# Twelve of the mixer's sixteen gate tiles as block products: seven products in place of eight, and the modulation rows moved

## The chip, the cores and the metric

The kernel runs on one core of a Trainium2 chip. The metric is the device time of one execution in microseconds, the median of several runs. One profiled execution gives the trace that is read here. Times inside the trace count from the start of its span.

## The reference

One decoder block over 512 tokens of width 1024, in float32. Three sub-layers follow each other, each behind an RMSNorm that is modulated by rows of `cond @ w_ada` (9 x 1024 values): a SwiGLU feed-forward part, a token mixer, a second feed-forward part; then a last RMSNorm.

```python
mod = cond @ w_ada[l] + b_ada[l]                       # nine vectors: shift, scale, gate, three times
u = modulate(rmsnorm(h, g_norm_ffn1[l]), sh1, sc1)
h = h + 0.5 * gt1 * swiglu(u, w_ffn1_in[l], w_ffn1_out[l])
u = modulate(rmsnorm(h, g_norm_mix[l]), sh2, sc2)
h = h + gt2 * token_mixing(u, ...)
...
# token_mixing
proj = u @ w_in                                        # pool 256, q 768, k 768, v 768, gates 2 x 1024
...
gates = sigmoid(gate_logits); g_pool, g_attn = split(gates, 2)
merged = g_pool * (y_pool @ w_pool_branch) + g_attn * (y_attn @ w_attn_branch)
return merged @ w_out
```

The gates are 2048 columns of `u @ w_in`: sixteen tiles of 128 columns, eight for `g_pool` and eight for `g_attn`.

## The kernel before

**Layout and precision.** Activations lie transposed: 1024 features as eight tiles of 128 partitions by 512 tokens. A float32 product is made of three matmuls: every operand is split into a hi part and a lo part, and `mm3` (L340) multiplies hi by hi, hi by lo and lo by hi into one PSUM bank. So a tile of 128 output columns (`mm_tile`, L1011) takes 8 x 3 matmuls of 512 columns. `UH` and `UL` hold the two parts of the normalised input, `MH` and `ML` those of the merged tiles.

**Weights.** Every weight chunk (128 x 1024 float32, 512 KB) is fetched by a DMA on SP's queue (`fetch`, L218) into one of three buffers `raw`, and is then split: `split_hi` (L274) lets ScalarE copy it to a ring `whi`, `split_lo` (L305) lets VectorE subtract that and write `wlo`. `look(n)` (L320) issues the splits n chunks ahead of the one that is taken. The buffer comes free when VectorE has done the lo part. The order in which the program is written is the order on every engine; the engines run on by themselves and wait for each other's results.

**Block products.** Most of the two feed-forward parts already use a scheme with seven products instead of eight (`duo`, L733): features and tokens are cut in two halves, four weight tiles in four blocks r11, r12, r22, r21, and sums and differences of the blocks are multiplied. A product (L720) has 24 matmuls of 256 columns. The sums of the weights are made by VectorE (`make`, L237) when a chunk is split; the order of a duo's seven entries is written in `blocks` (L167): r11, x0 = r12 - r11, x1 = r22 - x0, r21, r12 - r22, r22, x0 = r21 - x1. The sums of the activations are made once per sub-layer and split into `S`. Three PSUM banks A, B, C collect the seven products in the order A, B, A, C, A, B, A, and ScalarE copies A out (to C, to an SBUF tile) between the products. A settling matmul (L348) of 240 columns stands where matmuls of 512 columns give way to matmuls of 256.

**The mixer** (`mix`, L1195) goes: four q/k tiles of the first attention group together with the norm (`head`), the first group's values, eight q/k tiles of the dilated groups, two pool tiles, four value tiles, four gate tiles, then `merge_out` (L1327). Attention is hung into these tiles by `hooks` (L1259): at the sixth of the eight k steps of a tile stand the values of the block before last, the transposes of the last one, the scores of the next one and its softmax (maxima on VectorE, exponentials on ScalarE). Behind each q/k tile stands the rope (`rope_a`, L993: ScalarE copies the bank, four DMAs on SP's queue swap halves, VectorE multiplies by the cosine; `rope_b`, L1005: VectorE multiplies the swapped half by the sine and adds), its second half at the seventh step of the tile after.

**The merge.** `merge_out` makes the other twelve gate tiles, two for each merged tile m, each with `mm_tile`, and for every m the branches: twelve matmuls of 512 columns into two banks, then on VectorE two multiplications with the gates (L1355, L1356) and an addition (L1357), on ScalarE the hi part (L1358), on VectorE the lo part (L1359). Then comes the last product, `merged @ w_out`, with the out tail (`out_tail`).

**Modulation rows.** The 72 rows of 128 values of `mod` are made by VectorE, one instruction per row over a 512 KB tile of `w_ada` (`ada_do`, L364), fetched on SP's queue (`ada_fetch`, L357). `bg` (L388) does one row and fetches the next. Rows 48 to 71 are made in `merge_out`, two beside each of the twelve gate tiles, from a pool of four buffers. `AR` and `cs` are two 128 x 1024 tiles that hold norm sums and the rope's cosine and sine.

## Time and profile before

| what | us |
|---|---|
| time, median of 3 runs (997.77 to 998.7) | 998.47 |
| the profiled execution | 998.29 |
| its span in the trace | 996.5 |
| TensorE busy | 988.0 |
| VectorE busy | 746.8 |
| ScalarE busy | 456.9 |
| GpSimd busy | 26.8 |

The granted clock of TensorE was 1.00. In the rows of a timeline the columns are: start in us, duration in us, engine, line of the program, operation, output and inputs, shapes, count; in brackets the idle time of the engine ahead of it and what ended that. A matmul's duration is that of its pipelined passage; the distance of two starts is its price. In rows that sum a window: its length, then busy time and count for TensorE, its weight loads, VectorE, ScalarE and GpSimd, then the granted clock, the DMA share and GB/s. In rows of DMA issues: count, KB each, median us from issue to landing.

### The profile page before, as it was taken

What the parts mean: (1) busy time and instruction counts of PE and PEld (TensorE: products, weight loads), DVE (VectorE), ACT (ScalarE), POOL (GpSimd) and SP (SyncE); (2) the same over time, 40 slices, a digit from 0 to 9 for tenths busy, and PEclk for the clock granted to TensorE, in tenths of its full rate; (3) what the DMA queues carried; (4) which work ended last, traced back from release to release, by engine and by line L of the source; (5) the groups of instructions that cost most, each with busy time, mean ns of one, the idle gap of its engine ahead of it and who ended that gap; (6) DMA issues with size and microseconds to landing.
All of it is one profiled execution on the core that took longest, in us unless ns stands there. A gap on an engine that the chain in (4) does not pass through costs nothing.

```text
span 996.5 us, 15853 instructions
## 1 busy us (share of the span) xinstructions
PE 988.0 (99%) x6467; PEld 889.3 (89%) x6467; DVE 746.8 (75%) x1051; ACT 456.9 (46%) x690; POOL 26.8 (3%) x31
## 2 busy tenths in 40 slices
PE   9999999999999999999999999999999999999997
PEld 7888999989999999788878888998899899998997
DVE  7989979889797675776457776568797776676764
ACT  5443643625444454356432323464355254352553
POOL 0000000000000000008000000000000000000002
PEclk9999999999999999999999999999999999999999
DMA  9856446354564314433146663312343234241312
GB/s 345 276 195 224 149 149 210 134 197 160 190 186 124 120 61 123 127 104 119 44 148 241 233 236 125 106 65 81 111 149 128 64 107 147 86 148 43 105 45 85
DMA packets 44873, 141.70 MB, mean 142 GB/s; under 512 B 6273, under 2 KB 9089, under 8 KB 44802
## 3 DMA queue, kind: packets, MB, share of 16 engines
q1 hardware_dynamic: 44226, 140.18, 42.5%
q8 instruction: 50, 0.82, 0.3%
q10 hardware_dynamic: 576, 0.52, 0.2%
q14 instruction: 21, 0.17, 0.0%
HBM read 135.29 MB, written 2.24 MB: 138 GB/s over the span
## 4 chain that ended last, share of the span: by engine, by line
PE 95%; DVE 2%; DMA 1%; issue 1%; POOL 0%; ACT 0%; SPq 0%; POOLq 0%; DVEq 0%; ACTq 0%
PE bank L342 17%; PE bank L343 17%; PE bank L344 17%; PE bank L729 11%; PE bank L730 11%; PE bank L731 11%; PE bank L1541 2%; PE bank L1543 1%; PE bank L1545 1%; PE bank L1046 1%; PE bank L1305 1%; PE bank L1097 1%; PE bank L1306 1%; PE bank L1307 1%; PE bank L1079 1%; DMA H<-xT 1%
## 5 line engine op out<-in xcount | busy, mean ns | idle before, releaser
L311 DVE TENSOR_TENSOR wlo<-raw,whi 128x1024 fp32r<-128x1024 f32 (+5 forms) x171 | 175.7, 1040 | 65.6 <-ACT whi L299 64.9
L299 ACT ACTIVATE whi<-raw 128x1024 fp32r<-128x1024 f32 (+5 forms) x171 | 150.4, 898 | 47.3 <-DVE raw L243 43.9
L729 PE MATMUL bank<-UH,whi 128*128 128x256 f32 x544 | 150.2, 276 | 0.0
L730 PE MATMUL bank<-UL,whi 128*128 128x256 f32 x544 | 150.2, 276 | 0.0
L731 PE MATMUL bank<-UH,wlo 128*128 128x256 f32 x544 | 150.2, 276 | 0.0
L342 PE MATMUL bank<-HI,whi 128*128 128x512 f32 (+1 forms) x406 | 146.2, 360 | 0.0
L343 PE MATMUL bank<-HK,whi 128*128 128x512 f32 (+1 forms) x406 | 145.9, 359 | 0.0
L344 PE MATMUL bank<-HI,wlo 128*128 128x512 f32 (+1 forms) x406 | 145.8, 359 | 0.0
L342 PE MATMUL bank<-UH,whi 128*128 128x512 f32 (+1 forms) x400 | 143.0, 358 | 0.0
L343 PE MATMUL bank<-UL,whi 128*128 128x512 f32 (+1 forms) x400 | 141.6, 354 | 0.1
L344 PE MATMUL bank<-UH,wlo 128*128 128x512 f32 (+1 forms) x400 | 141.4, 354 | 0.0
L311 DVE TENSOR_TENSOR wlo<-X,whi 128x1024 fp32r<-128x1024 f32 (+4 forms) x101 | 111.8, 1112 | 32.1 <-ACT whi L299 31.9
L729 PE MATMUL bank<-SH,whi 128*128 128x256 f32 x408 | 112.7, 276 | 0.0
L730 PE MATMUL bank<-SL,whi 128*128 128x256 f32 x408 | 112.6, 276 | 0.0
L731 PE MATMUL bank<-SH,wlo 128*128 128x256 f32 x408 | 112.6, 276 | 0.0
L299 ACT ACTIVATE whi<-X 128x1024 fp32r<-128x1024 f32 (+4 forms) x101 | 95.5, 966 | 34.2 <-DVE X L243 33.5
L729 PEld LDWEIGHTS bank<-UH,whi 128*128 128x128 f32 x544 | 102.1, 188 | 0.3
L730 PEld LDWEIGHTS bank<-UL,whi 128*128 128x128 f32 x544 | 102.1, 188 | 0.0
L731 PEld LDWEIGHTS bank<-UH,wlo 128*128 128x128 f32 x544 | 102.1, 188 | 0.0
L344 PEld LDWEIGHTS bank<-HI,wlo 128*128 128x128 f32 x406 | 76.2, 188 | 11.7
L342 PEld LDWEIGHTS bank<-HI,whi 128*128 128x128 f32 x406 | 76.2, 188 | 11.5
L343 PEld LDWEIGHTS bank<-HK,whi 128*128 128x128 f32 x406 | 76.3, 188 | 11.3
(252 smaller groups left out, 1714.0 us busy)
## 6 DMA issues: line engine op xcount, KB each, us to landing
ada<-wada SPq DMA_DIRECT2D x47, 512.0 KB, 5.4
raw<-wmix SPq DMA_DIRECT2D x44, 512.0 KB, 3.7
raw<-wf1i SPq DMA_DIRECT2D x31, 512.0 KB, 4.3
raw<-wf2i SPq DMA_DIRECT2D x30, 512.0 KB, 3.6
X<-wf2i SPq DMA_DIRECT2D x14, 512.0 KB, 3.9
cs<-wada SPq DMA_DIRECT2D x12, 512.0 KB, 3.5
AR<-wada SPq DMA_DIRECT2D x12, 512.0 KB, 4.1
X<-wf1i SPq DMA_DIRECT2D x12, 512.0 KB, 4.4
```

The costliest lines, as they stand in the source:

```text
L299: self.nc.scalar.activation(self.hi[:, y], r[:, x], AF.Copy)
L311: self.nc.vector.tensor_tensor(self.lo[:, y], r[:, x], self.hi[:, y], op=OP.subtract)
L342: M(ps, hi, uh, start=start, stop=False)
L343: M(ps, hi, ul, start=False, stop=False)
L344: M(ps, lo, uh, start=False, stop=stop)
L729: M(o, hi, uh, start=start and p == 0 and k == 0, stop=False, skip_group_check=True)
L730: M(o, hi, ul, start=False, stop=False, skip_group_check=True)
L731: M(o, lo, uh, start=False, stop=k == 3, skip_group_check=True)
L1046: nc.tensor.matmul(S[:, o], q[:, toks], k[:, ks], start=True, stop=True, skip_group_check=True)
L1079: nc.tensor.transpose(b[:, i * P:i * P + P], p[:, i * P:i * P + P], self.ident)
L1097: self.nc.tensor.matmul(self.bO[64 * h:64 * h + 64, P * hp:P * hp + P], x, pt[:, (2 * h + j) * P:(2 * h + j + 1) * P], start=j == first, s ...
L1541: M(b, hi, self.UH[k], start=k == 0, stop=False)
```

## The change

Merged tiles are made in the order 6, 7, 0, 1, 2, 3, 4, 5. Tiles 6 and 7 have their four gate tiles as before, ahead of the merge. For the pairs (0, 1), (2, 3), (4, 5) the four gate tiles become one `gate_duo`: a settling matmul and seven products, with a copy of the feed-forward's bank scheme and two sigmoid tiles `gs` and `gc` for the four gates. The weights of these tiles are laid out as blocks. In `merge_out` a fourth `raw` buffer is added and `AR` and `cs` serve as x0 and x1. The activation sums are made by `mix_sums` in ten steps, which stand as hooks in the last value tile and three gate tiles; their tiles take the place of q, k and v tiles that are no longer read, as do the merged tiles. The pool that held the modulation rows' buffers in the merge is gone: rows 48 to 64 are made beside attention (one per q/k tile and in the first pool tile, two in the second pool tile and in three value tiles; buffer `AR`, from the second pool tile on also `cs`), rows 65 to 71 behind the first five tiles of the last product.

```diff
@@ lay_mix, plan
-    for m in range(KT + 1):
-        if m < KT:
-            ch.append(_fmajor(w_in, 2560 + np.arange(m * P, (m + 1) * P)))
-            ch.append(_fmajor(w_in, 3584 + np.arange(m * P, (m + 1) * P)))
...
+    for j in MERGED[::2]:
+        if j < KT - 2:
+            ch.extend(_blocks(w_in, *GATES, j))
...
+MERGED = (6, 7, 0, 1, 2, 3, 4, 5)
+GATES = (2560, 3584)
...
-        plain(mx)
+        plain(mx[:26])
+        for i in range(26, len(mx) - KT, 6):
+            blocks(mx[i:i + 4])
+            plain(mx[i + 4:i + 6])
+        plain(mx[-KT:])
@@ mix_sums (new): ten steps on VectorE and ScalarE, and last()
+        def last():
+            u = x[0].rearrange("p (k t) -> p k t", k=4)
+            nc.scalar.activation(self.S[3][0], u, AF.Copy)
+            sub(self.S[3][1], u, self.S[3][0])
...
+        return [lambda: whole(b, 0, 1), lambda: whole(x[0], 4, 1),
+                lambda: (v.tensor_tensor(x[0], x[0], b, op=OP.add), hi(0)), lambda: whole(x[1], 0, 0),
+                lambda: sub(x[2], x[1], b), lambda: (sub(x[1], x[0], x[1]), lo(0)),
+                lambda: (hi(2), whole(x[0], 4, 0)), lambda: (hi(1), sub(x[0], x[0], x[1])), lambda: lo(2), lambda: lo(1)], last
@@ mix
+            self.ada_free, self.ada_stop, self.ada_depth = [self.AR], 65, 2
+            self.bg_fetch()
...
-                        b = self.mm_tile(hooks(todo.pop(0), rest))
+                        b = self.mm_tile(hooks(todo.pop(0), rest + [(7, self.bg)]))
...
-            b = self.mm_tile(hooks([], rest + [(6, lambda: by_class(0))]))
+            b = self.mm_tile(hooks([], rest + [(6, lambda: by_class(0)), (7, self.bg)]))
             self.pool_diff(0, b)
-            b = self.mm_tile(hooks(g23[0], [(2, lambda: by_class(1))]))
+            self.ada_free.append(self.cs)
+            self.bg_fetch()
+            b = self.mm_tile(hooks(g23[0], [(2, lambda: by_class(1)), (3, self.bg), (7, self.bg)]))
...
-                hk = hooks(g23[c + 1], (), mid) if c < 3 else hooks([], [(2, self.at_swap)])
+                hk = hooks(g23[c + 1], [(2, self.bg), (7, self.bg)], mid) if c < 3 else \
+                    hooks([], [(2, self.at_swap), (2, nxt), (3, nxt), (6, nxt), (7, nxt)])
...
-            gates.append(self.mm_tile({6: [self.pool_map, lambda: self.at_fT(self.bS[1])]}))
+            gates.append(self.mm_tile({1: [nxt], 3: [nxt], 6: [self.pool_map, lambda: self.at_fT(self.bS[1])]}))
...
@@ gate_duo (new)
+        for i, (bank, u, start) in enumerate(((A, lambda: blk(lo4, T1), True), (B, lambda: S(0), True),
+                                              (A, lambda: S(1), False), (C, lambda: blk(hi4, T1), False),
+                                              (A, lambda: S(2), False), (B, lambda: S(3), False),
+                                              (A, lambda: blk(hi4, T2), False))):
+            if i == 6:
+                v.tensor_tensor(q(c, 1), q(c, 1), r(p5), op=OP.add)
+            self.look(4)
+            self.product(bank, u(), start, not i)
+            if i == 0:
+                copy(C, A)
+                if last:
+                    last()
+            elif i == 1:
+                copy(p5, B)
+            elif i == 2:
+                copy(q(c, 0), r(A))
+            elif i == 3:
+                sig(q(s, 0), r(C))
+            elif i == 4:
+                copy(q(c, 1), r(A))
+            elif i == 6:
+                sig(q(s, 1), r(A))
+                v.tensor_tensor(q(c, 0), r(B), q(c, 0), op=OP.add)
+        sig(c, c)
@@ merge_out
-            for m in range(KT):
-                if 0 < m < KT - 1:
-                    for _ in range(2):
-                        gates.append(sig(self.mm_tile()))
-                        self.bg()
-                        self.bg()
...
+            p5, raw = mg.tile([P, T], F32, name="p5"), mg.tile([P, D], F32, name="raw")
+            self.free.append(raw)
+            self.X, self.retired = [self.AR, self.cs], []
+            self.ready = True
...
+            for j in MERGED[::2]:
+                if j < 6:
...
+                    self.gate_duo(*sc, p5, last)
+                    last = None
+                for m in (j, j + 1):
...
+                    branch(m)
...
+            self.ada_free, self.ada_stop = [ma.tile([P, D], F32, name=x) for x in ("k0", "k2")], 72
+            self.bg_fetch()
...
                 self.sumsq(m, self.H[m])()
+                self.bg()
+                if m < 2:
+                    self.bg()
```

`branch(m)` is the body of the former loop over m, from `look()` to the lo part.

## The prediction

> **What bounds the kernel now.** I read the page first (shares, then the chain that ended last), then the timelines of the mixer's last third, engine by engine.

> ```profile
> PE 988.0 (99%) x6467; PEld 889.3 (89%) x6467; DVE 746.8 (75%) x1051; ACT 456.9 (46%) x690; POOL 26.8 (3%) x31
> ...
> PE 95%; DVE 2%; DMA 1%; issue 1%; POOL 0%; ACT 0%; SPq 0%; POOLq 0%; DVEq 0%; ACTq 0%
> ```

> TensorE is busy for 99% of the span and makes up 95% of the chain: nearly every microsecond of matmul that goes is a microsecond of time, and nearly every new wait of TensorE is one too. No other engine is near its limit on average, so the question is where the changed order makes TensorE wait. The price of a matmul, from the timeline of TensorE, in the mixer's merge and in the second feed-forward part:

> ```profile
> 520.07 0.39 PE L342 MATMUL bank<-UH,whi 128*128 128x512 f32 x1
> ...
> 530.95 0.39 PE L342 MATMUL bank<-PH,whi 128*128 128x512 f32 x1
> ...
> 716.45 0.27 PE L348 MATMUL bank<-UH,whi 128*128 128x240 f32 x1
> 716.56 0.28 PE L729 MATMUL bank<-UH,whi 128*128 128x256 f32 x1
> ...
> 735.61 0.28 PE L729 MATMUL bank<-UH,whi 128*128 128x256 f32 x1
> ```

> From 520.07 to 530.95 stand two gate tiles, 48 matmuls of 512 columns: 0.2267 us each (the 0.39 of a row is the pipelined length, not the price). From 716.56 to 735.61 stands one duo, the seven block products: 168 matmuls of 256 columns in 19.05, 0.1134 each, 2.72 a product. The 240-column settling matmul in front of it takes 0.11.

> **1. The removed matmuls.** Three times, four gate tiles (96 x 0.2267 = 21.76) become a settling matmul and a duo (19.16). Saved: 3 x 2.60 = 7.8 us, all on the path. The built program has 219 matmul instructions more, which is 3 x (168 - 96 + 1): the change does what it says. The weights are as many bytes as before.

> **2. A new wait in each gate duo.** In `gate_duo`, product 0 is accumulated in bank A, ScalarE copies A to C, and product 2 accumulates onto A again: it must wait for that copy. The copy is queued on ScalarE behind the two weight splits that `look(4)` issued ahead of product 0 (`branch` had looked ahead by 3 only). The second of them reads r12-r22, a subtraction that VectorE has behind the last `ML` of the branch before. Feed-forward 1 shows the same link once, at its first duo:

> ```profile
> 111.41 1.22 DVE L243 TENSOR_TENSOR X<-X 128x1024 f32<-128x1024 f32 x1
> ```
> ```profile
> 112.67 1.07 ACT L299 ACTIVATE whi<-X 128x1024 fp32r<-128x1024 f32 x1 [1.72 <-DVE X L243]
> 113.63 0.58 ACT L736 ACTIVATE u<-bank 128x512 f32<-128x512 f32 x1
> ```
> ```profile
> 114.27 0.38 PE L729 MATMUL bank<-SH,whi 128*128 128x256 f32 x1
> 114.49 0.28 PE L730 MATMUL bank<-SL,whi 128*128 128x256 f32 x1
> ```

> Subtraction to split 1.26, split to copy 0.96, copy 0.58 long, TensorE 0.06 after its end; and the first matmul after the wait takes 0.22 instead of 0.11. What comes ahead of the subtraction is read from a branch of the kernel as it is, which ends on TensorE at 547.27:

> ```profile
> 547.27 0.39 PE L342 MATMUL bank<-UH,whi 128*128 128x512 f32 x1
> ```
> ```profile
> 547.47 0.69 DVE L1356 TENSOR_TENSOR sg<-sg,bank 128x512 f32<-128x512 f32 x1 [0.22 <-PE bank L344]
> 548.19 0.69 DVE L1357 TENSOR_TENSOR sg<-sg 128x512 f32<-128x512 f32 x1
> 549.59 0.69 DVE L1359 TENSOR_TENSOR ML<-sg,MH 128x512 fp32r<-128x512 f32 x1 [0.70 <-ACT MH L1358]
> 550.54 1.23 DVE L311 TENSOR_TENSOR wlo<-raw,whi 128x1024 fp32r<-128x1024 f32 x1 [0.26 <-ACT whi L299]
> 551.68 1.22 DVE L369 SCALAR_TENSOR_TENSOR ada<-ada,cond 128x1024 f32<-128x1024 f32 x1
> ```
> ```profile
> 548.92 0.63 ACT L1358 ACTIVATE MH<-sg 128x512 fp32r<-128x512 f32 x1 [2.99 <-DVE sg L1357]
> 549.46 1.05 ACT L299 ACTIVATE whi<-raw 128x1024 fp32r<-128x1024 f32 x1
> ```

> Counted from the end of the pair's first branch: second multiplication at 0.20, `MH` 1.65, `ML` 2.32; the next chunk's lo part must wait for its hi part, queued on ScalarE behind `MH`, so it starts at 3.27 and leaves VectorE free at 4.41. The second branch ends at 2.72, but VectorE takes its first multiplication only at 4.41, the second 0.61 later at 5.02; then, by the same steps, `MH` at 6.47, `ML` at 7.14, the subtraction at 7.74, the split at 9.00, the copy from 9.96 to 10.54, TensorE at 10.60. Product 2 could start at 2.72 + 0.11 + 2 x 2.72 = 8.27. Wait: 2.33 + 0.11 = 2.4 us, in the second and third duo. At the first it is longer. There ScalarE has a table load and four sigmoids to do first, and in the kernel as it is takes its next split at

> ```profile
> 518.65 0.65 ACT L299 ACTIVATE whi<-raw 128x512 fp32r<-128x512 f32 x1
> ```

> In the changed one this is chunk r12-r11 and its lo part stands ahead of the branch's multiplications: 518.65 + 1.08 + 1.14 = 520.87 for the first, 521.48 for the second, against 520.07 + 0.20: 1.2 later. So 3.6. The three: 8.4 us. Floor, if the lo part does not hold VectorE up: the second multiplication at 2.92, 0.3 a duo, 1.0 in all. Later products have margins: the other copies stand behind one split each; the copy of product 2, worked out the same way, has 0.5 us left in the first duo and 2 in the others. As a bound on throughput VectorE is not it: a group takes 11 operations of 1.14 (551.68 less 550.54) and 12 of about 0.61, 19.9 us, of 19.16 + 5.44.

> **3. Modulation rows beside attention.** 17 rows, each a 512 KB DMA on SP's queue and one VectorE instruction of 1.22 (row 551.68), now stand at the end of the q/k tiles, with one buffer (AR) until the pool tiles. On SP the row's DMA waits for VectorE to be done with the row before, and the four rope DMAs of the tile (L1000) are queued behind it. Rope's second half waits for those, and the next row stands behind that on VectorE: a loop.

> ```profile
> 397.64 2.41 SPq L1000 DMA_DIRECT2D rt<-tr  x4
> 400.16 0.52 SPq L227 DMA_DIRECT2D raw<-wmix  x1
> 403.09 2.41 SPq L1000 DMA_DIRECT2D rt<-rt  x4
> ```
> ```profile
> 401.64 0.69 DVE L1008 TENSOR_TENSOR rt<-rt,cs 128x512 f32<-128x512 f32 x1 [1.79 <-DMA rt<-tr]
> 402.37 1.09 DVE L1009 TENSOR_TENSOR q<-q,rt 128x512 f32<-128x512 f32 x1
> 403.39 1.05 DVE L1002 TENSOR_TENSOR q<-bank,cs 128x512 f32<-128x512 f32 x1
> ```
> ```profile
> AR<-wada SPq DMA_DIRECT2D x12, 512.0 KB, 4.1
> ```

> Issue of a 512 KB row 0.5 (row 400.16), rope DMAs to rope 4.0 (397.64 to 401.64; I take 3.9, since four issues are done after 2.41), rope's two steps 1.75, the row 1.22: 7.4 us a turn. The first row that is late ends at 401.64 + 1.75 + 1.22 = 404.6, six turns later at 449.0, and the last rope starts 4.4 after that, at 453.4, and ends at 455.2. The next row then runs to 456.4, and the one after it stands at k = 3 of the second pool tile, in the same buffer: its DMA lands 4.1 later, at 460.5, it ends at 461.7. Behind it on VectorE stands the softmax of the first dilated scores.

> ```profile
> 454.35 1.09 PE bank L1046 x16
> ...
> 461.19 0.88 PE bank L1079 x8
> ```
> ```profile
> 455.47 0.42 DVE L1062 CUSTOM_DVE_ANT_0 prob<-bank,masks 128x256 f32<-128x256 f32 x1 [1.55 <-PE bank L1046]
> ```
> ```profile
> 458.49 0.50 ACT L1067 ACTIVATE prob<-prob,negmax 128x256 f32<-128x256 f32 x1
> ```

> The scores (454.35) would wait 0.9 for the rope. The last exponential ended 3.5 after VectorE's first maximum (455.47 to 458.99): now at 465.2. The second half of the transposes was due at 461.6. Wait in all 3.6, the 0.9 in it. Floor: nothing, if a turn takes no longer than a tile (from 403.09, the end of the second q/k tile, to the scores at 454.35, five of eight steps into the tenth tile, lie 7.6 tiles, 6.7 us each). Upper end: if the rope's pieces land only when the 512 KB in front of them has, a turn grows by about 1 us, and seven turns and the last row by 8: 12. I take 3.6; the loop's terms are all rows.

> **4. The rest, at nothing.** The ten steps of `mix_sums` (eleven VectorE instructions of 1.14, three of ScalarE) lie beside the last value tile and three gate tiles:

> ```profile
> 468.00:496.00 28.00, 28.00 (x200) 23.37 (x199) 12.14 (x32) 13.46 (x28) 5.98 (x6) 1.00 0.16 49
> 496.00:513.00 17.00, 17.00 (x81) 12.46 (x80) 10.01 (x23) 4.15 (x8) 0.00 (x0) 1.00 0.33 101
> ```

> VectorE is idle there for 23 of 45 us; the steps take 12.5, the rows of the value tiles 8. Cover gone: about 1 us at the transposition of the merge factors. The last seven rows stand behind the first five tiles of the last product; the third and fourth wait some 3 us for their buffers, but the weights of the next four tiles (5.4 us each) are split by then. The 24 rows that leave the merge give nothing back by themselves: TensorE did not wait there.

> **Sum.** -7.8 + 8.4 + 3.6 = +4.2 us. The profiled execution took 998.29 (span 996.5, 1.8 outside it), 0.18 under the median of 998.47; forecast 998.47 + 4.2 = 1002.7. About 0.2%, 2 us, can be told from no change.

> **Rivals.**
> A, the forecast, 45%: 1002.7, own range 999.5 to 1006.
> B, rows and ropes land in time and attention doesn't wait: +0.6, 999.1. For it: 6.7 us a tile against 7.4 a turn is a close call. 19%.
> C, the rope's pieces queue behind the rows' bytes: attention waits 6 to 12, 1005 to 1011. For it: one queue; against it: a row lands 4.1 after its issue, about when the last rope piece would land anyway. 9%.
> D, TensorE waits nowhere new: 998.47 - 7.8 = 990.7, the faster side. Mechanism: VectorE takes the second branch's multiplications without waiting for the lo part, and the copy comes in time; it decides at 2.3 us of slack a duo, and attention's at 3.6. For it: TensorE waits nowhere now, and at the one place shown the feed-forward duo loses 0.1. 13%.
> E, only the duos are at their floor: -7.8 + 1.0 + 3.6, 995.3. 11%.
> F, a wait makes the granted clock fall, 3%:

> ```profile
> 991.00:995.00 4.00, 0.10 (x1) 0.00 (x0) 1.76 (x6) 0.39 (x1) 1.41 (x2) 1.00 0.75 254
> ```

> Here TensorE has nothing to do from 991.10 on and the clock is still 1.00 at 995: 3.9 us idle did no harm, more than either long wait (3.6). Were it halved during one product after each of the two, that is 2 x 2.7 us more: 1008. [...]

> **How the numbers follow.** Faster by over 0.2%: D and E, 0.24. Within: most of B and the low end of A, 0.21. Slower: the rest, 0.55. The range leaves out D and the upper half of C: 994 to 1008; the likeliest case's own is given above.

> **What would show it.** Right: seven products of 19.05 a duo; a wait of TensorE for ScalarE's copy at the first matmul of the third product in each duo, 3.6, 2.4, 2.4; a wait at the first transposes of dilated attention, with a VectorE row waiting for its DMA just ahead. Wrong: no such waits, a copy that ends before product 1 does, or matmuls of 256 columns at more than 0.1134. A new wait in the last product or at the merge factors would upset step 4.

## The result and the profile after

The changed kernel took 1019.96 us (median of 4 runs, 1018.91 to 1021.9) against 998.23 for the kernel before: ratio 1.022, interval 1.0202 to 1.0238. It is slower by 21.7 us where 4.2 were forecast, and outside the range. The profiled execution (1021.9, span 1020.1) shows the same: 23.6 us more span. All windows and waits below are of that execution unless another kernel is named.

The page, shares and chain:

```profile
PE 993.1 (97%) x6686; PEld 900.9 (88%) x6686; DVE 788.6 (77%) x1091; ACT 475.6 (47%) x713; POOL 30.2 (3%) x31
...
PE 85%; DVE 6%; ACT 3%; DMA 2%; issue 2%; SPq 1%; POOL 0%; POOLq 0%; DVEq 0%; ACTq 0%
```

TensorE's share of the chain fell from 95% to 85%; VectorE, ScalarE and the DMAs have taken the rest. So there are places now where TensorE waits for them. The waits of TensorE (total us, times, longest):

```profile
PE bank L742 <- ACT bank L1396: 7.7, 3, 3.5
PE bank L1091 <- DVE k L1054: 4.5, 1, 4.5
PE bank L1142 <- DVE v L1375: 3.0, 1, 3.0
PE bank L1124 <- ACT prob L1112: 2.6, 2, 2.0
```

The first row is the three gate duos, the other three are attention: the scores that wait for the rope, the values that wait for VectorE's copy of the first value tile, the transposes that wait for the softmax. And behind some waits the granted clock is lower (window, its length, busy times of the engines, then the granted clock):

```profile
446.60:449.90 3.30, 3.30 (x9) 2.56 (x8) 3.30 (x5) 1.87 (x3) 0.00 (x0) 0.50 0.10 10
466.50:470.40 3.90, 3.90 (x10) 3.08 (x10) 2.64 (x3) 0.00 (x0) 3.75 (x4) 0.50 0.37 119
...
547.90:551.50 3.60, 0.16 (x2) 0.00 (x0) 3.47 (x4) 2.65 (x6) 0.00 (x0) 1.00 0.01 2
551.60:555.60 4.00, 4.00 (x22) 4.00 (x23) 3.66 (x4) 3.00 (x4) 0.00 (x0) 0.60 0.27 66
...
580.90:584.90 4.00, 4.00 (x36) 4.00 (x37) 4.00 (x4) 3.37 (x5) 0.00 (x0) 1.00 0.32 74
```

In the wait from 547.90 on TensorE does nothing and the clock reads 1.00; in the 4 us behind it, when the matmuls are back, it reads 0.60, with 22 matmuls of 256 columns where 36 fit (the window after the second duo's wait). When exactly it falls is shown at the experiment clock.

Where the 23.6 us come from, by setting the starts of the same matmuls in both traces side by side:

| part | us |
|---|---|
| removed matmuls (as forecast) | -7.8 |
| three waits in the duos, 3.7, 2.4, 2.1, and 0.1 for each restart | +8.6 |
| four waits in attention, 2.2, 4.7, 0.7, 3.1 | +10.7 |
| transposes one by one behind the exponentials, 0.9 twice | +1.8 |
| lower clock behind the waits: 5.4 in attention, 1.6 behind the first duo's | +7.0 |
| some products of 256 columns at 118 ns a matmul in place of 113 | about +2.6 |
| not assigned | about +0.7 |

The loss of the transposes is no matter of the clock, which reads 1.00 there. Eight of them, first in the kernel before, then in the changed one:

```profile
441.14 1.04 PE L1079 MATMUL bank<-cst,prob 128*128 128x128 f32 x8
```
```profile
444.56 1.92 PE L1124 MATMUL bank<-cst,prob 128*128 128x128 f32 x8 [2.04 <-ACT prob L1112]
```

In the changed kernel two of them start every 0.49 us, as far apart as the exponentials that they read (443.91, 444.42, 444.91 and 445.40 on ScalarE).

### The profile page after: what moved, and what is told of

Read it like the earlier page. It is cut to its first block, busy times and chain, and to the rows that moved or that the text cites. A ratio compares the mean times of both kernels' runs of the same rounds, so it can differ in the third digit from the quotient of the medians.

```text
span 1020.1 us, 16353 instructions
## 1 busy us (share of the span) xinstructions
PE 993.1 (97%) x6686; PEld 900.9 (88%) x6686; DVE 788.6 (77%) x1091; ACT 475.6 (47%) x713; POOL 30.2 (3%) x31
## 4 chain that ended last, share of the span: by engine, by line
PE 85%; DVE 6%; ACT 3%; DMA 2%; issue 2%; SPq 1%; POOL 0%; POOLq 0%; DVEq 0%; ACTq 0%
PE bank L355 13%; PE bank L356 13%; PE bank L357 13%; PE bank L742 12%; PE bank L743 12%; PE bank L744 12%; PE bank L1669 1%; PE bank L1671 1%; PE bank L1673 1%; DMA rt<-rt 1%; ACT whi L312 1%; DVE AR L382 1%; DVE wlo L324 1%; SPq L1045 1%; DMA rt<-tr 1%
## 5 line engine op out<-in xcount | busy, mean ns | idle before, releaser
L324 DVE TENSOR_TENSOR wlo<-raw,whi 128x1024 fp32r<-128x1024 f32 (+4 forms) x168 | 175.3, 1056 | 54.3 <-ACT whi L312 53.7
L742 PE MATMUL bank<-UH,whi 128*128 128x256 f32 x640 | 177.2, 277 | 0.0
L743 PE MATMUL bank<-UL,whi 128*128 128x256 f32 x640 | 177.2, 277 | 0.0
L744 PE MATMUL bank<-UH,wlo 128*128 128x256 f32 x640 | 177.1, 277 | 0.0
L312 ACT ACTIVATE whi<-raw 128x1024 fp32r<-128x1024 f32 (+4 forms) x168 | 149.9, 910 | 51.7 <-DVE raw L256 47.6
L324 DVE TENSOR_TENSOR wlo<-X,whi 128x1024 fp32r<-128x1024 f32 (+3 forms) x104 | 111.8, 1083 | 32.4 <-ACT whi L312 32.1
L312 ACT ACTIVATE whi<-X 128x1024 fp32r<-128x1024 f32 (+3 forms) x104 | 95.8, 943 | 33.6 <-DVE X L256 32.9
L355 PE MATMUL bank<-UH,whi 128*128 128x512 f32 (+1 forms) x304 | 107.2, 353 | 0.0
L356 PE MATMUL bank<-UL,whi 128*128 128x512 f32 (+1 forms) x304 | 105.8, 348 | 0.1
L357 PE MATMUL bank<-UH,wlo 128*128 128x512 f32 (+1 forms) x304 | 105.6, 347 | 0.0
L356 PEld LDWEIGHTS bank<-HK,whi 128*128 128x128 f32 x406 | 76.3, 188 | 11.3
## 6 DMA issues: line engine op xcount, KB each, us to landing
raw<-wmix SPq DMA_DIRECT2D x44, 512.0 KB, 3.8
raw<-wf1i SPq DMA_DIRECT2D x31, 512.0 KB, 4.5
raw<-wf2i SPq DMA_DIRECT2D x30, 512.0 KB, 4.1
AR<-wada SPq DMA_DIRECT2D x25, 512.0 KB, 4.2
ada<-wada SPq DMA_DIRECT2D x23, 512.0 KB, 5.7
cs<-wada SPq DMA_DIRECT2D x16, 512.0 KB, 3.6
X<-wf2i SPq DMA_DIRECT2D x14, 512.0 KB, 3.7
X<-wf1i SPq DMA_DIRECT2D x12, 512.0 KB, 4.4
```

The lines of the kernel that those rows point to most:

```text
L312: self.nc.scalar.activation(self.hi[:, y], r[:, x], AF.Copy)
L324: self.nc.vector.tensor_tensor(self.lo[:, y], r[:, x], self.hi[:, y], op=OP.subtract)
L355: M(ps, hi, uh, start=start, stop=False)
L356: M(ps, hi, ul, start=False, stop=False)
L357: M(ps, lo, uh, start=False, stop=stop)
L742: M(o, hi, uh, start=start and p == 0 and k == 0, stop=False, skip_group_check=True)
```

## The experiments

Times are medians, with the ratio to the kernel before, run in turn on the same chip (998.4 to 999.0). Single runs of one changed kernel differ by up to 0.6%, those of the kernel before by up to 0.3%.

**no_rows: attention without the rows.**

```diff
+            if not 48 <= j < 65:
                 self.nc.sync.dma_start(t[:, c], self.a["wada"][j * P:(j + 1) * P, c])
...
+            x = self.cond if 48 <= j < 65 else t
+            if 48 <= j < 65:
+                c = slice(0, 32)
```

> The 17 modulation rows beside attention are left out: their DMAs are gone and their VectorE instruction works on 32 columns of another tile (rows 48 to 64 of mod are not computed). Theory (the rows are the whole of attention's loss): the aligned traces lose 18.1 us between the first dilated q/k tiles and the merge; all of it goes, 1020.0 - 18.1 = 1001.9, own range 1000.5 to 1003.5, no wait of TensorE over 0.8 us in attention, granted clock 1.00 there. The duos keep their waits of 3.7, 2.4 and 2.1. Rival (the ten steps of the activation sums, or VectorE's load as such, hold a part): attention keeps 4 us or more, over 1006.

1003.22 us (1.0041, 1.0029 to 1.0053). The profiled run has no wait in attention; the duos' stay:

```profile
PE bank L746 <- ACT bank L1400: 7.7, 3, 3.5
```

By the starts of the same matmuls the changed kernel loses 18.3 us in attention against the kernel before, and no_rows loses nothing there. So all of it is the rows' doing, and the sums of `mix_sums` cost TensorE nothing there.

**rope_first: the same rows, another order on the queue.** `bg(False)` does a row and fetches none:

```diff
-                        b = self.mm_tile(hooks(todo.pop(0), rest + [(7, self.bg)]))
+                        b = self.mm_tile(hooks(todo.pop(0), rest + [(7, lambda: self.bg(False))]))
                         rt = [self.scratch(2 * i + hp)[:, :T] for i in range(2)]
                         self.rope_a(b, dst, hp, 4, *rt)
+                        self.bg_fetch()
```

> Only the order on the DMA queue: beside the eight dilated q/k tiles the four rope DMAs are issued ahead of the next row's fetch. Theory 1 (the loop through the queue): the rope no longer waits for the row before it, a tile keeps its 6.7 us, the waits at 442 (2.2) and 461 (4.7) go with the lower clock behind each (2.3 and 2.1): 1020.0 - 11.3 = 1008.7, 1006.5 to 1011; the waits at 474 (0.7) and 483 (3.2) stay. Theory 2 (VectorE has no time for a row in a q/k tile, whatever the queue does): the waits stay within 1 us, 1018 to 1021. Theory 3 (a row that comes later holds VectorE up instead): a VectorE row waits over 1 us for its DMA in each tile, 1012 to 1018.

1005.63 us (1.0068, 1.0051 to 1.0084): 14.3 less, where theory 1 gave 11.3; of the 3.0 more, 1.6 is the wait at 474, which went too (0.7, and 0.9 at its transposes). One wait stays in attention, 3.2 at the value tile. SP's queue and VectorE's rows, first of the changed kernel, then of rope_first:

```profile
423.30 0.33 SPq L374 DMA_DIRECT2D AR<-wada  x1
423.74 2.41 SPq L1045 DMA_DIRECT2D rt<-rt  x4
...
431.78 0.33 SPq L374 DMA_DIRECT2D AR<-wada  x1
```
```profile
428.79 0.69 DVE L1053 TENSOR_TENSOR rt<-rt,cs 128x512 f32<-128x512 f32 x1 [1.30 <-DMA rt<-rt]
...
430.52 1.22 DVE L382 SCALAR_TENSOR_TENSOR AR<-AR,cond 128x1024 f32<-128x1024 f32 x1
```
```profile
426.11 2.41 SPq L1046 DMA_DIRECT2D rt<-tr  x4
428.62 0.53 SPq L374 DMA_DIRECT2D AR<-wada  x1
```
```profile
430.06 0.69 DVE L1054 TENSOR_TENSOR rt<-rt,cs 128x512 f32<-128x512 f32 x1 [0.77 <-DMA rt<-tr]
...
432.20 1.23 DVE L382 SCALAR_TENSOR_TENSOR AR<-AR,cond 128x1024 f32<-128x1024 f32 x1 [0.33 <-DMA AR<-wada]
```

In the changed kernel a fetch comes every 8.48 us (423.30, 431.78), and the rope's pieces land 5.05 after their issue (423.74 to 428.79). With the rope first they land after 3.95 (426.11 to 430.06), the loop is broken, and theory 2 falls: VectorE has time for a row in a tile of 6.7 us. Theory 3 is seen but small: the row waits 0.33 for its DMA.

**eighth: the same order, an eighth of the bytes.**

```diff
+            if 48 <= j < 65:
+                c = slice(0, D // 8)
             self.nc.sync.dma_start(t[:, c], self.a["wada"][j * P:(j + 1) * P, c])
```

> The DMAs of the 17 rows beside attention bring an eighth of the row (64 KB in place of 512 KB), at the same place of the queue; VectorE's instruction keeps its size but reads another tile (rows 48 to 64 of mod are not computed). Theory 1 (bytes: the rope's pieces land late because 512 KB go ahead of them): the pieces land 3.9 to 4.1 us after the first issue, not 5.05, the turn of the loop falls from 8.45 to the 7.4 that was forecast; the wait at 461 shrinks from 4.7 to about 1 to 2 us, that at 442 to under 1, with less of the lower clock: 1005 to 1010. Theory 2 (the order of issue alone counts, not the bytes): the turn stays at 8.3 or more, 1017 to 1021.

1010.85 us (1.0128, 1.0102 to 1.0154), slightly above theory 1's range. In its trace:

```profile
427.30 0.33 SPq L376 DMA_DIRECT2D AR<-wada  x1
427.73 2.41 SPq L1048 DMA_DIRECT2D rt<-tr  x4
...
434.64 0.33 SPq L376 DMA_DIRECT2D AR<-wada  x1
```
```profile
431.68 0.69 DVE L1056 TENSOR_TENSOR rt<-rt,cs 128x512 f32<-128x512 f32 x1 [2.27 <-DMA rt<-tr]
```

The pieces land after 3.95, a turn takes 7.34: the loop as it was forecast (7.4), to 0.1. So the missing 1.1 us a turn is the 512 KB in front of the pieces, and TensorE's wait for the rope falls from 4.7 to 1.2; 1.9 at the transposes behind it take a part of that back.

**attn_fix: no rows before the first value tile's copy.** rope_first, and three rows moved into the gate tiles:

```diff
-            b = self.mm_tile(hooks(g23[0], [(2, lambda: by_class(1)), (3, self.bg), (7, self.bg)]))
+            b = self.mm_tile(hooks(g23[0], [(2, lambda: by_class(1)), (7, self.bg)]))
...
-                hk = hooks(g23[c + 1], [(2, self.bg), (7, self.bg)], mid) if c < 3 else \
+                hk = hooks(g23[c + 1], [(2, self.bg), (7, self.bg)] if c else [], mid) if c < 3 else \
...
```

> rope_first, and three rows moved: none at step 3 of the second pool tile and none in the first value tile; one each in the first three gate tiles. Theory (the 3.2 us that rope_first still lost stand for the rows ahead of VectorE's copy of the first value tile): that wait goes, 1005.6 - 3.2 = 1002.4, own range 1000.5 to 1004, the same as with no rows at all (1003.2). Rival (what waits there is GpSimd's pooling, which makes VectorE's instructions 2.1 long in place of 1.2, and not the rows): 1 to 2.5 us of it stay, 1003.5 to 1005.

1005.04 us (1.0068, 1.0054 to 1.0082): 0.6 less than rope_first, hardly a gain, and yet attention is clean, as with no rows at all. The time went to the next place where VectorE is full:

```profile
PE bank L743 <- ACT bank L1401: 10.9, 3, 6.7
```

The first duo's wait is 6.9 in place of 3.7: the rows in the gate tiles held up VectorE's steps ahead of the first branch. What VectorE does in the value tile of the changed kernel is shown by these rows:

```profile
478.81 2.08 DVE L382 SCALAR_TENSOR_TENSOR AR<-AR,cond 128x1024 f32<-128x1024 f32 x1
...
484.87 1.22 DVE L382 SCALAR_TENSOR_TENSOR cs<-cs,cond 128x1024 f32<-128x1024 f32 x1
...
486.01 0.69 DVE L1375 COPY v<-bank 128x512 f32<-128x512 f32 x1
```

The copy that TensorE waits for stands behind two rows, 2.08 and 1.22; with them moved away its wait of 3.2 is gone. The rival (GpSimd's pooling is the cause, and not the rows) falls, since the pooling runs in attn_fix too. But it may have a share: beside its first operations (L1214, 477.88 to 484.05 on GpSimd) the first row takes 2.08 where the second, behind them, takes 1.22, and a split between the two 2.06 where others take 1.22, together up to 1.7 of the wait.

**copy_first: ScalarE's copy ahead of the splits.**

```diff
-            self.look(4)
+            self.look(4 if i else 2)
             self.product(bank, u(), start, not i)
```

> Only the gate duo's order: product 0 looks 2 chunks ahead, not 4, so that ScalarE's copy of bank A stands ahead of the two splits. Theory (the copy behind the splits is the whole of the wait): the three waits (3.7, 2.4, 2.1), their restarts (0.3) and the time at a lower clock after the first (1.9) go, 10.3 us: 1009.7, own range 1008.5 to 1011. Rival (the wait only moves: the two splits come too late for products 3 and 4): a wait of 1 to 3 us at the first matmul of product 3 or 4 in each duo, 1013 to 1019.

1016.65 us (1.0181, 1.0166 to 1.0197): 3.3 less, not 10.3. Its waits in the duos:

```profile
PE bank L742 <- ACT gc L1396: 1.7, 3, 1.1
PE bank L744 <- DVE wlo L324: 1.3, 1, 1.3
...
PE bank L742 <- ACT bank L1396: 0.5, 1, 0.5
```

The waits at product 2 fell to 0.64, 0.47 and 0.44, so the splits were most of them, but in the first duo 1.4 and 1.3 came back at products 3 and 4, as the rival said. Starts of matmuls set side by side give 6.0 us for the duos in the two profiled runs; attention, with the same code, lost 2.5 more in this one than in the other.

**branch_look: the lo part out of the gap between the branches.**

```diff
-                self.look()
+                self.look(3 + (m % 2 == 0))
                 w = self.take()
                 pb, ab = self.nb(), self.nb()
```

> The changed kernel with one edit: the first branch of a pair looks 4 chunks ahead, so that VectorE's lo part of the second one no longer stands between the two branches; the two splits stay ahead of the copy. Theory (as forecast, the lo part between the branches is 1.5 us of each wait, the splits ahead of the copy the rest): the waits of the second and third duo fall from 2.4 and 2.1 to about 0.9 and 0.6; at the first, where VectorE starts late, the lo part only changes its place and 3.7 becomes 2.2 to 3.7; in all 3 to 6 us less, 1014 to 1017. Rival (the copy's own place behind the splits is nearly all): the waits stay above 1.8, 1019 to 1020.

1023.29 us (1.0245, 1.023 to 1.0261): both sides missed, it is 3.3 slower than the changed kernel. The waits are 3.3, 2.8 and 2.5, and the third now has 1.6 at a lower clock behind it. Ahead of the second duo's branches:

```profile
568.38 1.06 ACT L1404 ACTIVATE gc<-gc 128x1024 f32<-128x1024 f32 x1 [0.27 <-DVE gc L1427]
569.35 1.04 ACT L312 ACTIVATE whi<-cs 128x1024 fp32r<-128x1024 f32 x1
```
```profile
570.42 1.23 DVE L324 TENSOR_TENSOR wlo<-cs,whi 128x1024 fp32r<-128x1024 f32 x1 [2.07 <-ACT whi L312]
571.57 0.68 DVE L1455 TENSOR_TENSOR gs<-gs,bank 128x512 f32<-128x512 f32 x1
```

The lo part now waits for a hi part that stands behind the sigmoid of the duo before, VectorE is idle for 2.07, and the first branch starts at 571.57, 2.6 later than in the changed kernel against the same duo. What was taken out between the branches was put in ahead of both.

**duo_fix: the edits of copy_first and branch_look, and `last()` behind product 2.** The third edit:

```diff
                 copy(C, A)
-                if last:
-                    last()
             elif i == 1:
                 copy(p5, B)
             elif i == 2:
                 copy(q(c, 0), r(A))
+                if last:
+                    last()
```

> The gate duo again, with three orders changed: the copy of bank A ahead of the splits (as before), the weights of the second branch of a pair split ahead of the first branch's steps (the first branch looks 4 ahead), and the in-place sum that last() makes moved from product 0 to product 2. Theory (the wait is a queue: copy behind MH behind VectorE's lo part between the branches; copy_first took away only the splits): TensorE waits under 0.3 us at product 2 of each duo and under 0.3 at products 3 and 4, and the clock stays at 1.00 there: 10.3 us less than the changed kernel, 1009.7, own range 1008 to 1011.5. Rival (VectorE's load: it has 19.9 us of work in a group of 24.6 and the wait comes back wherever its queue is longest): 0.5 to 1.5 us a duo stay, 1012 to 1016.

1016.86 us (1.0172, 1.0155 to 1.0189), the rival's side, 0.9 above its range, and no better than copy_first. Set side by side the duos gain 6.2 us in the profiled run (1013.11, the fastest of the four); 2.9 of waiting are left, and they are ScalarE's copies behind splits once more, now also at product 4:

```profile
PE bank L742 <- ACT gc L1398: 1.9, 3, 0.7
PE bank L742 <- ACT bank L1398: 1.0, 2, 0.7
```

**both, best2, best3, best4: the whole computation, step by step.** `both` is duo_fix with attn_fix; the others move the rows on, and from best3 on the look-ahead of a duo's product is issued behind the copy that follows it (this edit alone is shown):

```diff
-            self.look(4 if i else 2)
             self.product(bank, u(), start, not i)
...
+            self.look()
         sig(c, c)
```

> duo_fix and attn_fix together, the whole computation done. Theory (the two waits and the lower clock behind them are all that stands against the removed matmuls): 1020.0 - 10.3 - 17.6 = 992.1; from the other side 998.5 - 7.8 = 990.7; so 990.5 to 993, faster than the kernel before by 0.6%. Rival (the waits share a cause, or a further one shows once they are gone): 995 to 1000.

999.76 us (1.0008, 0.9999 to 1.0017). Attention is clean; the first duo waits 3.8 for the three rows in the gate tiles, with 1.6 at a lower clock. The waits do share VectorE's time, so the rival holds.

> As both, but the three rows that both had in the gate tiles now stand behind the third to fifth tile of the last product (two rows per tile there). Theory (in both the three rows held VectorE up ahead of the first duo: its first branch was multiplied 2.8 us after TensorE's end, and TensorE waited 3.8 with 1.6 at a lower clock behind it): the first duo's wait falls to the 0.7 of duo_fix; 999.8 - 4.7 = 995.1, own range 993.5 to 996.5. Rival (the rows cost as much behind the last product, where VectorE has the weights of the last tiles to split): 997 to 1000.

1002.57 us (1.0033, 1.002 to 1.0045), worse, above both ranges. The first duo's wait at product 2 is cured (0.3), but the norm behind the last product waits 3.7 for VectorE, and a matmul of the last product 1.3 for a lo part.

> As best2, and in the gate duo the splits of each product's look-ahead are issued behind the copy that follows the product, not ahead of the product. Theory (the waits of 0.5 to 0.9 that duo_fix still had at product 4, and of 0.7 at product 2, are ScalarE's copies behind splits again): 2.5 of the 2.9 us left in the duos go, 1.5 to 3 us below best2, 991 to 994: faster than the kernel before by 0.5 to 0.8%. Rival (the splits come too late for their products instead): a wait for VectorE's lo part, no gain on best2.

998.71 us (1.0004, 0.9995 to 1.0013): 3.9 below best2, more than the 1.5 to 3 that were expected, and still above the range. The duos wait no more than 0.4 each. What is left:

```profile
PE bank L446 <- DVE AR L553: 2.8, 1, 2.8
```

This is the norm behind ten rows in the last product, and 1.2 at a lower clock behind it.

> As best3, with the modulation rows spread otherwise after attention: two in the third gate duo (behind products 4 and 6, in tiles of S that are read no more), eight behind the last product's first five tiles (best3 had ten there), three buffers. Theory (what best3 still loses, 3.0 us at the norm behind the last product and 1.2 at a lower clock behind it, is VectorE's backlog of ten rows): the wait falls below 0.7, 998.7 less 3 to 4.2: 994.5 to 995.7, faster than the kernel before by 0.3 to 0.45%. Rival (rows in the third duo bring its waits back): 996 to 999.

993.49 us (0.9947, 0.9934 to 0.9959): faster than the kernel before by 4.9 us, 26 less than the change as it was made, and 1.0 below the range. Its page:

```profile
PE 982.8 (99%) x6686; PEld 894.1 (90%) x6686; DVE 787.9 (79%) x1091; ACT 475.0 (48%) x713; POOL 29.5 (3%) x31
...
PE 88%; DVE 6%; ACT 2%; DMA 2%; issue 1%; POOL 0%; SPq 0%; POOLq 0%; ACTq 0%; DVEq 0%
```

TensorE is busy for 99% of the span again, with the same work on every engine. 2.9 us of the 7.8 are still missing. TensorE's waits of over 0.15 in the gate and merge part add up to 1.4 (0.3 and 0.4 in the first two duos, 0.7 at the start of the last product), and matmuls of 256 columns at 118 ns cost about 1.1 more than in the kernel before; the rest was not traced further.

**clock: what a wait costs behind it.** The kernel before, with n further copies on ScalarE in each duo of the second feed-forward part:

```diff
             if i == 0:
+                for _ in range((7, 8, 9, 10, 11, 12, 8, 9, 10, 9, 10)[j // 2] if hasattr(self, "f2") else 0):
+                    copy(p5, A)
                 copy(C, A)
```

> The kernel before, with 7, 8, 9, 10, 11, 12, 8, 9, 10, 9, 10 further copies of bank A on ScalarE ahead of the copy in the eleven duos of the second feed-forward part (their result is overwritten): TensorE waits about 1.6, 2.1, 2.6, 3.1, 3.6, 4.1, 2.1, 2.6, 3.1, 2.6, 3.1 us for it. Theory 1 (a length decides: so far a wait of 3.7 was always followed by matmuls at half speed for about 4 us, one of 2.1 never): all waits over about 3 are followed by it, none under 2.4. Theory 2 (the place in a grid of fixed windows decides, since waits of 2.4 were followed by it once in four): among the waits of 2.1 to 3.1 some are and some are not, without order in their length. Theory 3 (it is not the wait but what TensorE does after it): none is.

Nine of the eleven pairs are duos; the first has n = 9, and their waits came out 1.0 to 1.5 us longer than meant. The time is 1054.87 us, of a single run. With the duos' waits of the other traces, which like these stand between dense matmuls:

| wait, us | how many | followed by matmuls at half speed |
|---|---|---|
| 2.13 to 2.14 | 5 | 0 |
| 2.41 to 2.76 | 7 | 2 (2.42 and 2.53) |
| 3.10 to 3.33 | 2 | 2 |
| 3.66 to 3.77 | 8 | 7 |
| 4.35 to 6.87 | 6 | 6 |

The fall behind the first duo's wait in the changed kernel cost 1.6 us; it lasted for 3.41 (552.38 to 555.79). Between 2.4 and 3.7 the length of the wait does not decide: 2.42 had a fall once in five, 3.66 was once without one. That is theory 2, and in the traces the falls lie on a grid. In the changed kernel's the clock falls at 446.57, 463.64, 487.53 and 552.38, which lie 17.07, 23.89 and 64.85 apart (5, 7 and 19 times 3.413, a twelfth of the 40.96 from the first to the third), and stays at half for 3.41, 6.83, 3.41 and 3.41. Its last fall in the mixer, row by row:

```profile
548.97:552.38 3.41, 0.80 (x7) 0.80 (x7) 3.23 (x4) 2.49 (x4) 0.00 (x0) 1.00 0.01 2
552.38:555.79 3.41, 3.41 (x19) 3.41 (x18) 3.26 (x3) 2.41 (x4) 0.00 (x0) 0.50 0.32 77
555.79:559.21 3.42, 3.42 (x31) 3.42 (x30) 2.15 (x3) 1.41 (x4) 0.00 (x0) 1.00 0.57 187
```

In the trace of clock it falls at 749.02, 776.33, 824.12, 851.42 and 895.80, among other times: 8, 14, 8 and 13 times 3.413 apart. Set against stretches of that length, two waits as long as each other (723.04 to 726.70 and 893.54 to 897.20) differ:

```profile
721.72:725.13 3.41, 1.49 (x14) 1.29 (x12) 0.00 (x0) 3.22 (x7) 0.00 (x0) 1.00 0.22 90
725.13:728.55 3.42, 1.85 (x16) 1.85 (x17) 0.90 (x1) 3.39 (x6) 0.00 (x0) 1.00 0.00 0
...
892.38:895.80 3.42, 1.32 (x12) 1.13 (x10) 0.00 (x0) 3.26 (x6) 0.00 (x0) 1.00 0.19 77
895.80:899.21 3.41, 2.01 (x9) 2.01 (x10) 1.06 (x1) 3.38 (x6) 0.00 (x0) 0.50 0.00 0
```

The first wait is shared by two stretches, TensorE is busy for 1.49 and 1.85 in them, and the clock stays. The second leaves only 1.32 of the first stretch, 61% idle, and the next one is at half speed from its start, with the wait still on. Counted off from their falls, the traces of the changed kernel and of the kernel before have 582 such stretches from 12 us on. In six of them TensorE was idle for 59% or more, and the next was at half speed each time; it was so too behind one of 46% (443.16 to 446.57, busy for 1.84, with transposes in it), and behind none of the others, which are all at 40% or less. So in these traces the place of a wait in time counts beside its length. How much idle time it takes is not shown: 46% was once enough, and 56%, in the stretch from 721.72 on, was not.

## Why the prediction was wrong, step by step

**1, the removed matmuls: not contradicted.** The trace shows the duos in place of the gate tiles, and best4 shows most of the gain once the waits are gone. A matmul of 256 columns costs 113.4 ns in most products; in some it is 118, which no row of before showed there.

**2, the wait in the duo: right, in cause, place and size.** Forecast 3.6, 2.4, 2.4; the matmuls' starts give 3.7, 2.4, 2.1 and 0.1 for the restart. The chain at the second duo, whose first branch ends at 570.09:

```profile
570.36 0.69 DVE L1456 TENSOR_TENSOR gc<-gc,bank 128x512 f32<-128x512 f32 x1 [0.67 <-PE bank L357]
...
573.48 1.22 DVE L324 TENSOR_TENSOR wlo<-cs,whi 128x1024 fp32r<-128x1024 f32 x1 [0.26 <-ACT whi L312]
574.62 0.68 DVE L1455 TENSOR_TENSOR gs<-gs,bank 128x512 f32<-128x512 f32 x1
...
577.94 1.22 DVE L256 TENSOR_TENSOR raw<-raw,raw 128x1024 f32<-128x1024 f32 x1
```
```profile
579.19 1.06 ACT L312 ACTIVATE whi<-raw 128x1024 fp32r<-128x1024 f32 x1 [0.85 <-DVE raw L256]
580.15 0.58 ACT L1396 ACTIVATE bank<-bank 128x512 f32<-128x512 f32 x1
```
```profile
580.78 0.39 PE L742 MATMUL bank<-v,whi 128*128 128x256 f32 x1 [2.25 <-ACT bank L1396]
```

Counted from 570.09 the lo part starts at 3.39, the second branch at 4.53, the subtraction at 7.85, the split at 9.10, the copy at 10.06 and TensorE at 10.69; forecast were 3.27, 4.41, 7.74, 9.00, 9.96 and 10.60. Steps added up from rows of an engine's queue hold to 0.1 us. The floor of 0.3 a duo was wrongly thought out: branch_look shows that the lo part does not vanish, it moves. In best4, where the copy stands ahead of the splits as well, 0.3 and 0.4 are left in two duos.

**3, the rows beside attention: the right loop, one term too short, and two places missed.** The turn was summed to 7.4 with 3.9 for the rope's landing; behind the row's 512 KB it is 5.05, and the turn 8.48. The step had this case as its upper end, a turn longer by about 1 us, and it was rival C, at 9%: its 6 to 12 us of waiting hold the 7.6 that the lag cost (2.2, 4.7 and 0.7; the 3.1 at the value tile belong to step 4). The reason given against it (a row lands 4.1 after its issue, about when the last piece would) was no reason: the pieces then land behind it. The lag therefore grew by 1.7 a tile in place of 0.7. It first stopped TensorE at the transposes at 444.56 (2.2), where the maxima of the scores stand behind the late rope and its row on VectorE:

```profile
437.49 0.69 DVE L1053 TENSOR_TENSOR rt<-rt,cs 128x512 f32<-128x512 f32 x1 [3.62 <-DMA rt<-tr]
...
439.19 1.22 DVE L382 SCALAR_TENSOR_TENSOR AR<-AR,cond 128x1024 f32<-128x1024 f32 x1
...
442.84 0.42 DVE L1107 CUSTOM_DVE_ANT_0 prob<-bank,masks 128x256 f32<-128x256 f32 x1
```

The prediction followed the lag only to the last rope. The scores lost 4.7 where 0.9 was forecast, and the first dilated transposes, where it saw the rest of its 3.6, lost 0.7 and 0.9.

**4, the cover of the value tiles: wrong.** VectorE's idle time (23 of 45 us) was enough on average, but the copy of the first value tile stands behind two rows in order: 3.2.

**F, the lower clock: 7.0 us, at a chance of 3%.** The sum left this term out; even C at its upper end, 1011, ended 9 below the result. The row that was held against it, clock 1.00 in 991 to 995 with TensorE idle, was read too early. The row behind it in the same trace, of the kernel before, reads 0.77:

```profile
995.00:996.40 1.40, 0.00 (x0) 0.00 (x0) 0.00 (x0) 0.00 (x0) 0.00 (x0) 0.77 0.07 23
```

In finer steps, up to the fall and behind it:

```profile
992.35:995.76 3.41, 0.00 (x0) 0.00 (x0) 0.41 (x2) 0.00 (x0) 0.66 (x1) 1.00 0.81 274
995.76:996.40 0.64, 0.00 (x0) 0.00 (x0) 0.00 (x0) 0.00 (x0) 0.00 (x0) 0.50 0.00 0
```

The clock falls to half at 995.76, 4.66 us after TensorE ran out of work. So this idle stretch did bring a fall; it cost nothing because no matmul came behind it. Behind the first duo's wait the fall cost 1.6, where the prediction reckoned with 2.7 behind each long one.

Sign and mechanism of the forecast hold; the size fails on the landing behind the bytes, on the waits in attention that were not followed, and on the clock. A to E left the clock out and F had the rope on time; the case that came was C and F together, which the list did not hold.

## What to carry to other kernels

When a background job gets one more DMA on a queue that also carries small transfers someone waits for, price the small ones behind its bytes (here they landed after 5.05 us in place of 3.95), and issue them first: here that order alone was worth 14 us. Follow a lag on an in-order engine to every operation queued there, not only to the one it began with, and price a wait of TensorE with a second part for the slower matmuls behind it: here the shortest wait between dense matmuls that had one was 2.42 us, and the six of 4.35 and more all had one. Moved work is cheap only where the engine is free at that moment: three rows moved from one place to the next cost some 3 to 7 us there, until a place with room was found.

## What was not expected of the hardware

```profile
463.70:465.60 1.90, 0.00 (x0) 0.00 (x0) 1.87 (x3) 0.00 (x0) 1.82 (x2) 0.50 0.01 4
```

Another came just behind one: the first duo's wait ended at 551.58, and the clock fell at 552.38. The row 547.90:551.50, which ends before that, reads 1.00 and hides it. Some products of 256 columns ran at 118 ns a matmul, others at 113, in the first feed-forward part for about 1.2 us of loss in the changed kernel's run and for none in that of no_rows, with the same code there; the cause stays open. The single runs of no_rows lie between 1000.1 and 1005.2; their mean granted clock goes with it, 0.997 in the fastest and 0.993 in the slowest. A difference of 0.004 over 1000 us is 4 us at most, so falls of the clock that come in some runs and not in others would explain most of the spread; the single falls were not traced.
